# Storing four rows of one image by transfers of 98, 10, 8, 6, 4 and 2 channels

## The chip, the core and the metric

The kernel runs on one core of a Trainium2 chip. The metric is the device time of one execution in microseconds (us); the kernel before took 126.87 us as the median of 3 runs (126.73 to 127.43). A core has a matrix engine (PE, with its weight loads PEld), two elementwise engines (DVE, ACT), a general one (POOL), a sequencer (SP) that here only issues transfers, and 16 DMA engines that move the data between device memory (HBM) and the on-chip buffer. SP and ACT issue stores, each on its own DMA queue: q1 belongs to SP, q10 to ACT; q0 belongs to POOL, which issues loads that also cast.

## The reference

A 3x3 convolution with padding 1 over 16 images of 64 input channels, 64 x 64 pixels, into 128 output channels, all in float32:

```
for kh in range(3):
    for kw in range(3):
        output[b, co] += weight[co, ci, kh, kw] * x_pad[b, ci, kh:kh+h, kw:kw+w]
```

The inputs are 16.8 MB and 0.3 MB, the output is 33.6 MB.

## The kernel before

The images are taken in eight pairs, `p` = 0 to 7; the 64 channels of two images fill the 128 partitions. A pair is computed in four blocks, `blk` = 0 to 3, of 16 output rows each. In each block PE makes three groups of products per image (L141): `U`, `A` and `Bt`. ACT copies `U` out of the accumulators (L155), and DVE adds `A` to it for the even output rows (L164) and `Bt` for the odd ones (L167). The sums go into `ots[0]` and `ots[1]`, the two output tiles of the pair, one an image: 128 partitions (output channels) of 16 KB, which are 64 rows of 256 bytes.

The pairs' inputs come by loads on POOL's queue (L58, six of them) and on SP's (L42, L46, L48); POOL also makes sums of input rows (L67). The last load is issued at 48.1 us.

What matters here is how the outputs leave. When block 3 of a pair is done, SP stores `ots[0]` whole (2 MB, L97); the store of `ots[1]` is kept in the list `held` and issued by ACT in the next block, after its copies of `U`. Only the last pair is stored in two halves, after blocks 1 and 3. Each of these 18 stores has 128 partitions, and each partition's bytes are one packet of a DMA engine: 16 KB, or 8 KB in the last pair. Each DMA engine gets 8 packets of every store.

Each engine, SP and ACT too, runs its instructions in the order of the program, so an instruction that waits holds all behind it. A transfer reports its landing on a semaphore. The layer that builds the program has eight of these for the transfers of SP and ACT, here called 0 to 7, and hands them out in turn in program order; a transfer that gets a semaphore for a second or third time waits, before it is issued, until the earlier transfer with the same one has landed. In the kernel before, 24 transfers share them: the six loads of SP take 0 to 5, pair 0 takes 6 and 7, pair 1 takes 0 and 1, and so on to pair 5 with 0 and 1, pair 6 with 2 and 3, and pair 7 with 4, 5, 6 and 7.

Of the kernel before, what the change touches and what calls it, by code (L numbers as in the profile page):

```python
# [12 lines left out]
@with_exitstack  # L13
def kernel(
    ctx: ExitStack,
    tc: tile.TileContext,
    x: bass.AP,
    weight: bass.AP,
    out: bass.AP,
):  # L20
    nc = tc.nc
    B, CI, H, W = x.shape
    CO = weight.shape[0]
    assert H == 64 and W == 64 and CI == 64 and CO == 128 and B % 2 == 0
    NP = B // 2
    RB = 8

    keep = tc.keep_in_program_order
    x_rows = x.rearrange("b c h w -> (b c) h w")
    out_rows = out.rearrange("b co h w -> b co h w")  # L30
    w_flat = weight.rearrange("co ci kh kw -> co (ci kh kw)")

    const = ctx.enter_context(tc.tile_pool(name="const", bufs=1))
    psum = ctx.enter_context(tc.tile_pool(name="psum", bufs=8, space=bass.MemoryType.PSUM))
    xpool = ctx.enter_context(tc.tile_pool(name="xpool", bufs=5))
    opool = ctx.enter_context(tc.tile_pool(name="opool", bufs=8))
    spool = ctx.enter_context(tc.tile_pool(name="spool", bufs=3))
    upool = ctx.enter_context(tc.tile_pool(name="upool", bufs=4))


    w_raw = const.tile([CO, CI * 9], F32)
    nc.sync.dma_start(w_raw, w_flat)  # L42
    x0 = opool.tile([128, H, W], F32, tag="ot", name="x0")
    cuts = [(0, 18), (18, 34), (34, 50), (50, 64)]
    for lo, hi in cuts:
        nc.sync.dma_start(x0[:, lo:hi, :], x_rows[0:128, lo:hi, :])  # L46
    x1 = opool.tile([128, H, W], F32, tag="ot", name="x1")
    nc.sync.dma_start(x1, x_rows[128:256, :, :])  # L48
    ident = const.tile([128, 128], F16)
    make_identity(nc, ident)  # L50
    w16 = const.tile([CO, CI * 9], F16)
    keep(nc.gpsimd.tensor_copy(w16, w_raw))  # L52

    xs = {p: xpool.tile([128, H, W], F16, tag="xs", name="xs") for p in (0, 1)}

    def load(p):
        xs[p] = xpool.tile([128, H, W], F16, tag="xs", name="xs")
        keep(nc.gpsimd.dma_start(xs[p], x_rows[128 * p : 128 * p + 128, :, :]))  # L58

    ss = {}  # L60

    def sums(eng, p, src, lo, n):
        if p not in ss:
            ss[p] = spool.tile([128, H // 2, W], F16, tag="ss", name="ss")
        v = src.rearrange("p (j i) c -> p j i c", i=2)
        keep(
            eng.tensor_add(  # L67
                ss[p][:, lo : lo + n, :], v[:, lo : lo + n, 0, :], v[:, lo : lo + n, 1, :]
            )
        )  # L70


    Wt = const.tile([128, 5, 3, CO], F16)
    G0, G21, G1, G01, G2 = range(5)

    def wrow(i):
        return Wt[:, i, :, :].rearrange("p t c -> p (t c)")

    for kh, g in ((1, G1), (2, G2), (0, G0)):
        wp = psum.tile([128, 512], F32, tag="acc", name="wp")  # L80
        for k in range(3):
            t = 3 * kh + k
            for q in (0, 64):
                nc.tensor.matmul(wp[q : q + 64, k * CO : k * CO + CO], w16[:, t::9], ident)  # L84
        keep(nc.scalar.copy(wrow(g), wp[:, 0 : 3 * CO]))  # L85
    keep(nc.gpsimd.tensor_sub(wrow(G21), wrow(G2), wrow(G1)))  # L86
    keep(nc.gpsimd.tensor_sub(wrow(G01), wrow(G0), wrow(G1)))  # L87
    for p in range(2, 5):
        load(p)
    for n, (lo, hi) in enumerate(cuts):  # L90
        sums(nc.vector, 0, x0, RB * n, RB)
        keep(nc.scalar.copy(xs[0][:, lo:hi, :], x0[:, lo:hi, :]))  # L92

    held = []

    def store(eng, p, b2, ot, lo, hi):
        return eng.dma_start(  # L97
            out_rows[2 * p + b2, :, lo:hi, :],
            ot.rearrange("p j i c -> p (j i) c")[:, lo:hi, :],
        )  # L100

    for p in range(NP):
        if p + 1 < NP:
            for lo in (0, 16):
                sums(nc.gpsimd, p + 1, x1 if p == 0 else xs[p + 1], lo, 16)
        if p > 0 and p + 4 < NP:
            load(p + 4)
        ots = [
            opool.tile([128, H // 2, 2, W], F32, tag="ot", name="ot") for _ in range(2)
        ]  # L110
        for blk in range(4):
            j0 = blk * RB

            def group(wi_rows):

                tiles = [
                    psum.tile([128, RB, W], F32, tag="acc", name="acc") for _ in range(2)
                ]
                n = 3 * len(wi_rows)
                i = 0  # L120
                for wi, off in wi_rows:
                    for kw in (1, 0, 2):
                        c_lo, c_hi = max(0, 1 - kw), min(W, W + 1 - kw)
                        for b2 in range(2):
                            p0 = 64 * b2
                            lo, hi = j0, j0 + RB
                            if off is None:
                                rhs = ss[p][p0 : p0 + 64, lo:hi, c_lo + kw - 1 : c_hi + kw - 1]
                            else:
                                while 2 * lo + off < 0:  # L130
                                    lo += 1
                                while 2 * (hi - 1) + off > H - 1:
                                    hi -= 1
                                first = 2 * lo + off
                                last = 2 * (hi - 1) + off
                                rhs = xs[p][
                                    p0 : p0 + 64,
                                    first : last + 1 : 2,
                                    c_lo + kw - 1 : c_hi + kw - 1,
                                ]  # L140
                            nc.tensor.matmul(  # L141
                                tiles[b2][:, lo - j0 : hi - j0, c_lo:c_hi],
                                Wt[p0 : p0 + 64, wi, kw, :],
                                rhs,
                                start=i == 0,
                                stop=i == n - 1,
                            )
                        i += 1
                return tiles

            U = group([(G1, None)])
            us = []
            for b2 in range(2):
                ut = upool.tile([128, RB, W], F32, tag="ut", name="ut")
                keep(nc.scalar.copy(ut, U[b2]))  # L155
                us.append(ut)
            if p == 0:
                for lo in {2: (0, 16), 3: (32, 48)}.get(blk, ()):
                    keep(nc.scalar.copy(xs[1][:, lo : lo + 16, :], x1[:, lo : lo + 16, :]))  # L159
            while held:  # L160
                keep(store(nc.scalar, *held.pop(0)))
            A = group([(G21, 1), (G0, -1)])
            for b2 in range(2):
                nc.vector.tensor_add(ots[b2][:, j0 : j0 + RB, 0, :], A[b2], us[b2])  # L164
            Bt = group([(G01, 0), (G2, 2)])
            for b2 in range(2):
                nc.vector.tensor_add(ots[b2][:, j0 : j0 + RB, 1, :], Bt[b2], us[b2])  # L167
            parts = {3: (0, 64)} if p < NP - 1 else {1: (0, 32), 3: (32, 64)}
            if blk in parts:
                lo, hi = parts[blk]  # L170
                store(nc.sync, p, 0, ots[0], lo, hi)
                held.append((p, 1, ots[1], lo, hi))
    while held:
        keep(store(nc.scalar, *held.pop(0)))

# [29 lines left out]
```

## Time and profile before

| | |
|---|---|
| median of 3 runs | 126.87 us |
| profiled execution | 126.71 us, of which its span is 124.9 us |
| PE | 106.1 us busy (85%), its last matmul before 112 us |
| DVE | 83.3 us (67%) |
| ACT | 44.6 us (36%) |
| POOL | 37.4 us (30%) |
| q1 (SP), q10 (ACT), q0 (POOL): share of the 16 DMA engines' span | 41.3%, 31.6%, 24.6% |
| HBM read and written | 17.07 MB and 33.55 MB |

The span runs from the first to the last instruction; 1.8 us of the execution's time lie around it. The page cuts the span into 40 equal slices and gives, for each engine, the busy share of a slice in tenths. For the DMA engines it gives the mean share of the 16. Windows of the trace give the same for stretches that one chooses, and the list of transfers gives the time from the issue of a transfer to its landing.

### The profile page before, as it was taken

How to read it: one execution, taken by the hardware profiler on the slowest of the kernel's cores; microseconds unless marked ns; L12 is line 12 of the kernel's file. 1: busy time of each engine (PE TensorE's matmuls, PEld its weight loads, DVE VectorE, ACT ScalarE, POOL GpSimd, SP SyncE). 2: the span in 40 equal slices, each digit the busy share in tenths (PEclk: the TensorE clock that was granted, in tenths of full speed). 3: DMA queues.
4: the chain of work that ended last, by engine and by line, in shares of the span. 5: the costliest groups of instructions: out<-in, count | busy, mean ns of one | idle time of the engine just before them, and what ended most of it. 6: DMA issues, size and time to landing. Idle time of an engine off the chain costs nothing.

```text
span 124.9 us, 2410 instructions
## 1 busy us (share of the span) xinstructions
PE 106.1 (85%) x978; PEld 53.9 (43%) x978; DVE 83.3 (67%) x132; ACT 44.6 (36%) x76; POOL 37.4 (30%) x29
## 2 busy tenths in 40 slices
PE   0489999999999999999999999999999999970000
PEld 0334455554555545455554554555545555430000
DVE  0066777877787778777877878887887787771000
ACT  4396379533333333333333333333333333320000
POOL 2293079995019401290005800084000000000000
PEclk9999999999999999999999999999999999996555
DMA  4999999999999999999999999999999999999992
GB/s 115 332 434 420 283 215 215 218 226 362 378 359 370 328 349 380 359 338 344 367 378 354 338 357 373 428 425 425 425 436 425 441 420 430 420 417 425 428 404 102
DMA packets 4330, 44.48 MB, mean 356 GB/s; under 512 B 480, under 2 KB 480, under 8 KB 1120
## 3 DMA queue, kind: packets, MB, share of 16 engines
q1 hardware_dynamic: 2160, 21.27, 41.3%
q10 hardware_dynamic: 1296, 16.78, 31.6%
q0 software_dynamic: 864, 6.29, 24.6%
q8 instruction: 7, 0.11, 0.3%
q14 instruction: 3, 0.02, 0.0%
HBM read 17.07 MB, written 33.55 MB: 405 GB/s over the span
## 4 chain that ended last, share of the span: by engine, by line
PE 83%; DMA 4%; DVE 2%; issue 1%; DVEq 0%; SPq 0%
PE acc L141 83%; DMA x<-in_x_dram 4%; DVE ot L164 1%; DVE ss L67 1%; DVE ot L167 0%; DVEq L200 0%; SPq L42 0%; DVEq L164 0%
## 5 line engine op out<-in xcount | busy, mean ns | idle before, releaser
L141 PE MATMUL acc<-xs,Wt 64*128 64x504 f16 (+3 forms) x768 | 88.9, 378 | 0.0
L141 PEld LDWEIGHTS <-Wt 64*128 64x128 f16 x960 | 52.8, 95 | 52.8 <-issue 3.3
L155 ACT COPY ut<-acc 128x512 f32<-128x512 f32 x64 | 34.4, 590 | 61.6 <-issue 42.8
L164 DVE TENSOR_TENSOR ot<-acc,ut 128x512 f32<-128x512 f32 x64 | 41.2, 686 | 22.3 <-PE acc L141 19.2
L167 DVE TENSOR_TENSOR ot<-acc,ut 128x512 f32<-128x512 f32 x64 | 41.2, 685 | 0.0
L67 POOL TENSOR_TENSOR ss<-xs 128x1024 f16<-128x1024 f16 x12 | 25.2, 2123 | 26.4 <-DMA xs<-in_x_dram 15.9
L141 PE MATMUL acc<-ss,Wt 64*128 64x504 f16 (+1 forms) x192 | 27.0, 384 | 1.0 <-DVE ss L67 1.0
L67 DVE TENSOR_TENSOR ss<-x 128x512 f16<-128x512 f32 x4 | 3.0, 741 | 7.3 <-DMA x<-in_x_dram 7.3
L58 POOL DMA_DIRECT2D xs<-in_x_dram x6 | 3.5, 580 | 11.6 <-PE acc L141 11.6
L67 POOL TENSOR_TENSOR ss<-x 128x1024 f16<-128x1024 f32 x2 | 4.7, 2366 | 5.8 <-DMA x<-in_x_dram 5.8
L84 PE MATMUL wp<-ident,w 128*64 128x128 f16 x18 | 1.3, 328 | 4.4 <-POOL w L52 4.4
L92 ACT CAST xs<-x 128x1024 f16<-128x1024 f32 (+2 forms) x4 | 4.1, 1058 | 0.2 <-DMA x<-in_x_dram 0.2
L159 ACT CAST xs<-x 128x1024 f16<-128x1024 f32 x4 | 4.0, 1059 | 0.0
L84 PEld LDWEIGHTS <-w 128*64 128x64 f16 x18 | 1.1, 210 | 4.4 <-POOL w L52 4.4
L85 ACT CAST Wt<-wp 128x384 f16<-128x384 f32 x3 | 1.2, 489 | 3.1 <-PE wp L84 3.1
L86 POOL TENSOR_TENSOR Wt<-Wt 128x384 f16<-128x384 f16 x1 | 1.4, 1439 | 1.7 <-ACT Wt L85 1.7
L85 ACT ACT_TABLE_LOAD x1 | 1.3, 1283 | 0.7 <-PEq L189 0.7
L52 POOL CAST w<-w_raw 128x576 f16<-128x576 f32 x1 | 0.7, 665 | 2.4 <-DMA w_raw<-in_weight_dram 2.4
L87 POOL TENSOR_TENSOR Wt<-Wt 128x384 f16<-128x384 f16 x1 | 1.4, 1353 | 0.0
masks.py:199 POOL TENSOR_SCALAR_AFFINE_SELECT ident<-ident 128x128 f16<-128x128 f16 x1 | 0.3, 293 | 0.1
masks.py:197 POOL MEMSET ident<- 128x128 f16 x1 | 0.2, 205 | 0.3 <-POOLq L189 0.3
L189 POOL MEMSET const-float32-0.0<- 128x1 f32 x1 | 0.1, 98 | 0.2 <-issue 0.2
(3 smaller groups left out, 0.3 us busy)
## 6 DMA issues: line engine op xcount, KB each, us to landing
out_dram<-ot SPq DMA_DIRECT2D x7, 2048.0 KB, 20.7
out_dram<-ot ACTq DMA_DIRECT2D x7, 2048.0 KB, 20.9
xs<-in_x_dram POOLq DMA_DIRECT2D x6, 1024.0 KB, 27.4
x<-in_x_dram SPq DMA_DIRECT2D x1, 2048.0 KB, 13.0
out_dram<-ot SPq DMA_DIRECT2D x2, 1024.0 KB, 12.2
out_dram<-ot ACTq DMA_DIRECT2D x2, 1024.0 KB, 12.0
x<-in_x_dram SPq DMA_DIRECT2D x2, 512.0 KB, 6.0
x<-in_x_dram SPq DMA_DIRECT2D x1, 576.0 KB, 4.8
```

The costliest lines, as they stand in the source:

```text
L58: keep(nc.gpsimd.dma_start(xs[p], x_rows[128 * p : 128 * p + 128, :, :]))
L67: eng.tensor_add(ss[p][:, lo : lo + n, :], v[:, lo : lo + n, 0, :], v[:, lo : lo + n, 1, :])
L84: nc.tensor.matmul(wp[q : q + 64, k * CO : k * CO + CO], w16[:, t::9], ident)
L85: keep(nc.scalar.copy(wrow(g), wp[:, 0 : 3 * CO]))
L86: keep(nc.gpsimd.tensor_sub(wrow(G21), wrow(G2), wrow(G1)))
L87: keep(nc.gpsimd.tensor_sub(wrow(G01), wrow(G0), wrow(G1)))
L92: keep(nc.scalar.copy(xs[0][:, lo:hi, :], x0[:, lo:hi, :]))
L141: nc.tensor.matmul(tiles[b2][:, lo - j0 : hi - j0, c_lo:c_hi], Wt[p0 : p0 + 64, wi, kw, :], rhs, start=i == 0, stop=i == n - 1,)
L155: keep(nc.scalar.copy(ut, U[b2]))
L159: keep(nc.scalar.copy(xs[1][:, lo : lo + 16, :], x1[:, lo : lo + 16, :]))
L164: nc.vector.tensor_add(ots[b2][:, j0 : j0 + RB, 0, :], A[b2], us[b2])
L167: nc.vector.tensor_add(ots[b2][:, j0 : j0 + RB, 1, :], Bt[b2], us[b2])
```

## The change

In pair 5 (`NP - 3`), the store of `ots[0]` leaves out rows 60 to 63, so each of its packets has 15 KB. These four rows, 1 KB in each of 128 partitions, are stored on SP's queue by six transfers of 98, 10, 8, 6, 4 and 2 partitions, written in the program after block 1 of pair 6. The store of `ots[1]` stays whole. No byte is added or left out.

```
-    def store(eng, p, b2, ot, lo, hi):
+    def store(eng, p, b2, ot, lo, hi, c_lo=0, c_hi=CO):
         return eng.dma_start(
-            out_rows[2 * p + b2, :, lo:hi, :],
-            ot.rearrange("p j i c -> p (j i) c")[:, lo:hi, :],
+            out_rows[2 * p + b2, c_lo:c_hi, lo:hi, :],
+            ot.rearrange("p j i c -> p (j i) c")[c_lo:c_hi, lo:hi, :],
         )
...
-            parts = {3: (0, 64)} if p < NP - 1 else {1: (0, 32), 3: (32, 64)}
+            if p == NP - 2 and blk == 1:
+                lo = 0
+                for n in (98, 10, 8, 6, 4, 2):
+                    store(nc.sync, *spread, 60, 64, lo, lo + n)
+                    lo += n
+            cut = (p, blk) == (NP - 3, 3)
+            if cut:
+                spread = (p, 0, ots[0])
+            parts = {3: (0, 60 if cut else 64)} if p < NP - 1 else {1: (0, 32), 3: (32, 64)}
             if blk in parts:
                 lo, hi = parts[blk]
                 store(nc.sync, p, 0, ots[0], lo, hi)
-                held.append((p, 1, ots[1], lo, hi))
+                held.append((p, 1, ots[1], lo, 64 if cut else hi))
```

PE, DVE, ACT and POOL keep their instructions in their order. SP has six more. The end of SP's list in the built program, from the store of pair 5 on, with what each transfer waits for (`DMAHW0` is completion semaphore 0, `DVE` the sums):

```
L97 DMACopy out_0_dram<-ot_1060 128x3840 [waits DMAHW0_49,DVE_49]
L97 DMACopy out_0_dram<-ot_1060 98x256 [waits DMAHW2_49]
L97 DMACopy out_0_dram<-ot_1060 10x256 [waits DMAHW3_49]
L97 DMACopy out_0_dram<-ot_1060 8x256 [waits DMAHW4_49]
L97 DMACopy out_0_dram<-ot_1060 6x256 [waits DMAHW5_49]
L97 DMACopy out_0_dram<-ot_1060 4x256 [waits DMAHW6_49]
L97 DMACopy out_0_dram<-ot_1060 2x256 [waits DMAHW7_49]
L97 DMACopy out_0_dram<-ot_1243 128x4096 [waits DMAHW0_49,DVE_49]
L97 DMACopy out_0_dram<-ot_1429 128x2048 [waits DMAHW2_49,DVE_49]
L97 DMACopy out_0_dram<-ot_1429 128x2048 [waits DMAHW4_49,DVE_49]
```

ACT's store of pair 5 has semaphore 1 as before, that of pair 6 now waits for semaphore 1 instead of 3, and those of pair 7 for 3 and 5 instead of 5 and 7.

## The prediction
> **What bounds the kernel now.** I read the page's chain first. It gives PE 83%, but it ends with the last DVE add at about 112.9 us, and the span is 124.9 us. So the last 12 us belong to something that the chain does not follow. The slices and the queues say what it is:
>
> ```profile
> PE   0489999999999999999999999999999999970000
> DMA  4999999999999999999999999999999999999992
> q1 hardware_dynamic: 2160, 21.27, 41.3%
> q10 hardware_dynamic: 1296, 16.78, 31.6%
> q0 software_dynamic: 864, 6.29, 24.6%
> ```
>
> The 16 DMA engines are busy in every slice, and the three queues add up to 97.5% of them. The kernel is bound by its transfers. The waits of SP's queue agree: at the end (L200) it waits for stores alone.
>
> ```profile
> SPq L97 <- DVE ot L167: 105.2, 9, 18.8
> SPq L200 <- DMA out_dram<-ot: 10.9, 6, 4.3
> ```
>
> Next the stores around the change: when each is issued (timeline: start, length), and how long it takes to land (list of transfers, each cut out by a window; the order below is pair 5 by SP and ACT, then the last halves by SP and ACT).
>
> ```profile
> 86.76 0.33 SPq L97 DMA_DIRECT2D out_dram<-ot  x1
> 87.36 0.34 ACTq L97 DMA_DIRECT2D out_dram<-ot  x1
> 99.56 13.14 SPq L97 DMA_DIRECT2D out_dram<-ot  x3
> 100.17 0.34 ACTq L97 DMA_DIRECT2D out_dram<-ot  x1
> ...
> out_dram<-ot SPq DMA_DIRECT2D x1, 2048.0 KB, 17.5
> out_dram<-ot ACTq DMA_DIRECT2D x1, 2048.0 KB, 17.8
> out_dram<-ot SPq DMA_DIRECT2D x1, 1024.0 KB, 11.4
> out_dram<-ot ACTq DMA_DIRECT2D x1, 1024.0 KB, 11.0
> ```
>
> Pair 5 lands at 86.76 + 17.5 = 104.26 us (SP) and 87.36 + 17.8 = 105.16 us (ACT). Pair 6 is issued at 99.56 (the first of the three in that row) and 100.17 us, 4.7 and 5.0 us before that. This lead keeps the DMA engines fed. The last store lands at 112.97 + 11.0 = 123.97 us. Last, windows (length, then five engines, granted clock, DMA share, GB/s):
>
> ```profile
> 0.00:1.70 1.70, 0.00 (x0) 0.00 (x0) 0.00 (x0) 0.97 (x1) 0.70 (x6) 1.00 0.00 0
> 1.70:1.80 0.10, 0.00 (x0) 0.00 (x0) 0.00 (x0) 0.10 (x1) 0.00 (x0) 1.00 0.96 115
> 115.00:120.00 5.00, 0.00 (x0) 0.00 (x0) 0.00 (x0) 0.00 (x0) 0.00 (x0) 0.50 1.01 428
> 120.00:121.00 1.00, 0.00 (x0) 0.00 (x0) 0.00 (x0) 0.00 (x0) 0.00 (x0) 0.50 0.99 418
> 121.00:122.00 1.00, 0.00 (x0) 0.00 (x0) 0.00 (x0) 0.00 (x0) 0.00 (x0) 0.50 0.83 352
> 122.00:123.00 1.00, 0.00 (x0) 0.00 (x0) 0.00 (x0) 0.00 (x0) 0.00 (x0) 0.50 0.49 205
> 123.00:124.00 1.00, 0.00 (x0) 0.00 (x0) 0.00 (x0) 0.00 (x0) 0.00 (x0) 0.50 0.10 41
> ```
>
> Three readings. Stores run at 428 GB/s. The 16 engines do not finish together: the shares after 120 us sum to 2.41 us, so the mean engine ends at 122.4 and the last at about 123.7 us. And a queue that was empty starts 1.0 us after its issue: SP's first load is issued at 0.74 us, and the DMA engines are idle until 1.7.
>
> **The change part by part.** *Fewer bytes in one store, six small ones.* The bytes stay 128 KB, that is 0.31 us of all engines at 428 GB/s. Packets go from 8 of 16 KB to 8 of 15 KB and, on the mean, 8 of 1 KB on each engine. From the trace's packets, 8 KB take 309 ns, 4608 bytes 178 and 2304 bytes 93, a slope of 37 ns per KB and about 8 ns fixed: 8 x 8 ns = 0.06 us on the mean engine. An engine that got none of the small packets would gain 0.30 us, one that got 12 would lose about 0.25. I take 0, between -0.30 and +0.25, because all of this is done by about 104 us and what follows wipes out who was ahead.
>
> Here a rule on which engines get the small packets stands by itself. The Trainium skill, "DMA: Bandwidth & Descriptors", section "Why a DMA increments its semaphore by 16 and not by 1", says that a transfer runs on the largest number of engines up to 16 that divides its partitions, the lowest-numbered ones: 14, 10, 8, 6, 4 and 2 engines here, so that the last two get nothing. The same page's table of latencies calls engines 7 and 15 usually slower; by both rules the change would unload a late engine and be worth about -0.3 us by itself, which no row of this profile can show, since its packets carry no engine numbers.
>
> *Six more issues on SP.* 6 x 0.33 us = 2.0 us on a queue that waits 105 us for DVE. Four can go at once after 86.76 us; the last two wait for semaphores 6 and 7, pair 4's stores, issued at 73.95 and 74.55 us and landing after 20.6 and 20.9 us, at 94.6 and 95.5 us. SP is through with them before its next work at 99.56 us: nothing.
>
> *The semaphores move by six.* This is the term that counts. In the kernel before, pair 6 waits for semaphores 2 and 3, last used by pair 2, long landed. In the changed one it waits for 0 and 1, which **pair 5** used. SP's store of pair 6, ready at 99.56 us, is held until SP's store of pair 5 has landed; ACT's, ready at 100.17, until ACT's has. The lead of 5 us is gone: the engines run dry of pair 5 before pair 6 is known to them.
>
> When do they restart? Pair 5's store lands at 104.26, earlier by its missing bytes on the engine that is last (8 x 37 ns = 0.3 us): 103.96. SP issues at 104.0 (in the kernel before it started 0.03 us after the add that freed it). First packets 1.0 us later, 105.0; on the last of the 16 engines about 105.2, as the first load's packets spread over 0.2 us. What is left is pairs 6 and 7, 8.39 MB / 428 GB/s = 19.6 us, gapless as before, ending at 124.6 to 124.8 us. The last landing came about 0.3 us after its last packet: 124.9 to 125.1. An instruction fetch of 8 KB (packets, at 111.2 us) adds 0.3 if it falls on the last engine: 124.9 to 125.4, middle 125.2, against 123.97. So +1.2 us.
>
> Note what that sum contains: the mean engine loses far more, from about 103.1 us (its end, 122.4, less 19.5) to 105.1, but the last engine, which sets the end, was due at 104.2 and loses only 1.0. After the restart all engines start level.
>
> The unknown in it is the latency from issue to first packet in mid-kernel. Lower bound 0.33 us, the length of the issue itself, before whose end no packet can be known to an engine: +0.5. Upper bound 2.2 us, the first load's whole flight (2.9 us in the page's list) less its bytes (288 KB, 0.7 us), with pair 5 landing at 104.26 without the 0.3 us gain: +2.7. I take 1.0, since that row is the same queue starting from empty engines, though at the program's start.
>
> The same skill page, section "Latency and other measured facts", gives about 0.6 us to the first byte of such a transfer; by that the sum would be +0.8 instead of +1.2. The row above shows 1.0, which decides.
>
> *ACT held.* Behind its held store stand the copies of `U` for block 1 of pair 7, due at 102.66 us. They start when ACT's store of pair 5 has landed (104.6 to 105.2) plus 0.34, about 105.3: 2.6 us late. DVE's adds of that block, due at 103.97, start about 1.9 late, after the first copy; four adds take 2.7 us of a block's 3.2 (PE's 103.65 us of the chain over 32 blocks), so two blocks later some 0.9 is left. The last stores are issued near 113.3 and 113.9 instead of 112.4 and 113.0. The DMA engines have work until 105.1 + 14.7 = 119.8 us by then (pair 6 and half of pair 7), so 5 us of cover: nothing.
>
> Sum: 126.71 + 1.2 = 127.9 us for an execution like the profiled one; the median stands 0.16 above it, so 128.1 us.
>
> **Rivals.** *A short gap, no measurable change.* A restart by 104.5 us or earlier (a start latency of 0.4 us) ends within 0.6 us of before, 126.3 to 127.5. For it: the late engines run to 104.2 anyway. Against it: the 1.0 us row. *Faster.* The unloading counts and the gap does not: 126.87 - 0.3 = 126.6. It decides only if the new packets are there by 104.2 us, when the last engine runs dry, so if pair 5's store lands by 103.2, 0.8 us earlier than I find. *Much slower by ACT.* If the held copies cost 5 us more than I count, the final halves reach dry queues: each further us is one us, 129 to 131. Against it: the 5 us of cover. *Much slower by the small transfers.* Should the 98 partitions go to one engine, 98 x 45 ns = 4.4 us land on it, ahead of pair 6 in its queue: 132. Nothing in the profile excludes it, as all transfers there have 128 partitions. *No wait at all* would need the program not to hold these stores; its list says that it does.
>
> **How the numbers follow.** The held stores with a loss of +0.5 to +2.7 us on the median of 126.87: 0.82, 127.4 to 129.6, with 128.1 inside; the lowest 0.1 us of that, within the bound below, is counted with the next case. Short gap: 0.08. Faster: 0.03. The two much slower: 0.07 together. The range 127.4 to 129.6 leaves the rest out. About 0.5% (0.6 us) is what a measurement of this kernel can tell: faster 0.03, within 0.08, slower 0.89.
>
> **What would show it.** In the profile after: the waits of SP's queue have a wait of L97 for a store of 4 to 5 us; pair 6's stores are issued near 104.0 and 105 us; a window near 103 to 105 us has a DMA share well under 0.9; ACT has a wait of about 5 us there; the shares after 121 us fall off steeply instead of over 3 us; the last store lands near 125.2 us. The prediction is wrong if pair 6 is issued near 99.6 us, if the dip is absent, or if the gap stays but the late engines are others than I think and lose 2 us or more.

## The result and the profile after

The changed kernel took 128.58 us as the median of 4 runs (128.41 to 128.84), beside 126.8 us for the kernel before (126.51 to 127.43). The ratio is 1.0138, with a 95% interval of 1.0104 to 1.0172: slower by about 1.8 us. The profiled execution took 128.67 us, 1.96 more than the profiled one of before; its span is 126.9 us.

The page of the changed kernel, slices and queues:

```profile
PE   0469999999999999999999999999999999920000
DMA  4999999999999999999999999999999949999992
q1 hardware_dynamic: 2332, 21.27, 40.9%
q10 hardware_dynamic: 1296, 16.78, 31.1%
q0 software_dynamic: 864, 6.29, 24.2%
```

The bytes of the three queues are the same; SP's queue has 172 packets more (128 of 1 KB and 44 reports of landing, one from each engine that took part in a small store: 14 + 10 + 8 + 6 + 4 + 2). One slice of the DMA row, the 33rd (101.5 to 104.7 us), has fallen from 9 to 4. Nothing else in that row has changed.

The waits of SP's queue after (who waited for what: us in total, times, longest):

```profile
SPq L97 <- DVE ot L167: 88.9, 8, 19.3
SPq L97 <- DMA out_dram<-ot: 14.1, 3, 8.3
SPq L208 <- DMA out_dram<-ot: 12.6, 6, 3.4
```

The second line is new: SP waits with a store for an earlier store. Its longest wait, 8.3 us, is that of pair 6's store. It began when the last small transfer was out, at about 95.7 us; the part that costs is what lies behind the 99.9 us at which the sums of pair 6 are ready, about 4.1 us.

The issues and flights around it (timeline of SP and ACT, then the list of transfers cut by windows: pair 5 by SP, by ACT, pair 6 by SP):

```profile
87.11 8.53 SPq L97 DMA_DIRECT2D out_dram<-ot  x7
104.04 0.36 SPq L97 DMA_DIRECT2D out_dram<-ot  x1
104.36 0.34 ACTq L97 DMA_DIRECT2D out_dram<-ot  x1
104.79 1.07 ACT L155 COPY ut<-acc 128x512 f32<-128x512 f32 x2 [3.88 <-DMA out_dram<-ot]
...
out_dram<-ot SPq DMA_DIRECT2D x1, 1920.0 KB, 16.9
out_dram<-ot ACTq DMA_DIRECT2D x1, 2048.0 KB, 16.6
out_dram<-ot SPq DMA_DIRECT2D x1, 2048.0 KB, 9.9
```

Pair 5 lands at 87.11 + 16.9 = 104.01 us (SP) and 87.71 + 16.6 = 104.3 us (ACT, issued at 87.71), and pair 6 is issued 0.03 to 0.06 us after each. Its flight is 9.9 us where it was 14.4: the queue is empty when it comes. Windows of the changed kernel (length, five engines, granted clock, DMA share, GB/s):

```profile
102.00:103.00 1.00, 1.00 (x14) 0.47 (x11) 1.00 (x3) 0.00 (x0) 0.00 (x0) 1.00 0.60 240
103.00:104.00 1.00, 1.00 (x12) 0.54 (x10) 0.60 (x2) 0.00 (x0) 0.00 (x0) 1.00 0.26 91
104.00:104.90 0.90, 0.90 (x12) 0.45 (x8) 0.00 (x0) 0.11 (x1) 0.00 (x0) 1.00 0.01 5
104.90:105.00 0.10, 0.10 (x4) 0.07 (x2) 0.00 (x0) 0.10 (x1) 0.00 (x0) 1.00 5.09 2130
...
123.00:124.00 1.00, 0.00 (x0) 0.00 (x0) 0.00 (x0) 0.00 (x0) 0.00 (x0) 0.50 1.07 451
124.00:125.00 1.00, 0.00 (x0) 0.00 (x0) 0.00 (x0) 0.00 (x0) 0.00 (x0) 0.50 0.41 172
125.00:126.00 1.00, 0.00 (x0) 0.00 (x0) 0.00 (x0) 0.00 (x0) 0.00 (x0) 0.50 0.02 8
```

(A packet is counted where it starts, so a short window can show more than 1.) The engines run dry one after another from 102 us on, the last of them just before 104.2 us, and nothing of weight moves until 104.9. Then all start within 0.15 us of each other, the first of them 0.86 us after the start of SP's issue. At the end they also stop together, between 124.5 and 124.8 us by the trace's packets, where in the kernel before they stopped over 2.4 us. But not all: 8 GB/s over the last window is one packet of 8 KB, so one engine goes on alone, to 125.5 us.

### The profile page after: what moved, and what is told of

It reads as the page before. It is cut to its first block, busy times and chain, and to the rows that moved or that the text cites. A ratio compares the mean times of both kernels' runs of the same rounds, so it can differ in the third digit from the quotient of the medians.

```text
span 126.9 us, 2416 instructions
## 1 busy us (share of the span) xinstructions
PE 105.7 (83%) x978; PEld 55.1 (43%) x978; DVE 84.1 (66%) x132; ACT 44.7 (35%) x76; POOL 36.8 (29%) x29
## 4 chain that ended last, share of the span: by engine, by line
PE 81%; DMA 4%; DVE 2%; issue 1%; DVEq 0%; SPq 0%
PE acc L141 81%; DMA x<-in_x_dram 4%; DVE ss L67 1%; DVE ot L164 1%; DVEq L208 0%; DVE ot L167 0%; SPq L42 0%; DVEq L164 0%
## 5 line engine op out<-in xcount | busy, mean ns | idle before, releaser
L141 PEld LDWEIGHTS <-Wt 64*128 64x128 f16 x960 | 53.9, 95 | 52.0 <-issue 3.6
L67 DVE TENSOR_TENSOR ss<-x 128x512 f16<-128x512 f32 x4 | 4.0, 1007 | 6.9 <-DMA x<-in_x_dram 6.8
L86 POOL TENSOR_TENSOR Wt<-Wt 128x384 f16<-128x384 f16 x1 | 0.9, 910 | 1.7 <-ACT Wt L85 1.7
L87 POOL TENSOR_TENSOR Wt<-Wt 128x384 f16<-128x384 f16 x1 | 1.4, 1358 | 0.0
## 6 DMA issues: line engine op xcount, KB each, us to landing
out_dram<-ot ACTq DMA_DIRECT2D x7, 2048.0 KB, 16.6
out_dram<-ot SPq DMA_DIRECT2D x1, 1920.0 KB, 16.9
```

Of the source, the lines that this page charges most:

```text
L67: eng.tensor_add(ss[p][:, lo : lo + n, :], v[:, lo : lo + n, 0, :], v[:, lo : lo + n, 1, :])
L141: nc.tensor.matmul(tiles[b2][:, lo - j0 : hi - j0, c_lo:c_hi], Wt[p0 : p0 + 64, wi, kw, :], rhs, start=i == 0, stop=i == n - 1,)
```

## The experiments

Two theories stand against each other. *Held stores*: the time goes because pair 6's stores wait, through the reused semaphores, until pair 5's have landed, and the queues run dry. *Small transfers*: the 1 KB packets, or their uneven shares on the engines, cost it. The first four kernels below ran beside a kernel before of 126.61 us (28 runs), the last three beside 126.77 us (23 runs).

### Four transfers: the semaphores move by four

```
-                for n in (98, 10, 8, 6, 4, 2):
+                for n in (98, 10, 8, 12):
```

> The same four rows by four transfers of 98, 10, 8 and 12 channels instead of six. The semaphores move by four, so pair 6 waits for those of pair 4 (landed by 95.5 us, before 99.6). Held stores (the loss comes from pair 6 waiting for pair 5 to land): no gap, 126.5 to 127.1 us, pair 6 issued near 99.6 and 100.2 us, no dip of the DMA share at 103 us. Small transfers (1 KB packets or their uneven shares cost the time): still 128 us or more.

Measured: 126.93 us, ratio 1.0042 (1.0025 to 1.0059). Its window from 102 to 106 us (under the next experiment) has no dip, and SP issues pair 6 when its sums are ready:

```profile
99.89 0.36 SPq L97 DMA_DIRECT2D out_dram<-ot  x1
```

Of the 1.4% that the six transfers cost, four of them leave 0.4%.

### Loads that nobody reads: only the semaphores move

```
+            if p == NP - 2 and blk == 1:
+                for n in range(6):
+                    tiny = const.tile([16, W], F32, name=f"tiny{n}")
+                    keep(nc.sync.dma_start(tiny, x_rows[0:16, n, :]))
             parts = {3: (0, 64)} if p < NP - 1 else {1: (0, 32), 3: (32, 64)}
             if blk in parts:
                 lo, hi = parts[blk]
-                store(nc.sync, p, 0, ots[0], lo, hi)
+                keep(store(nc.sync, p, 0, ots[0], lo, hi))
```

Made from the kernel before; `keep` holds SP's order as written.

> The store of pair 5 is whole, as in the kernel before; in place of the six small stores SP issues six loads of 4 KB (16 partitions of 256 bytes) that nothing reads. Only the semaphores move, by six. Held stores: the gap is back, 128.2 to 128.9 us, pair 6 issued near 104.3 and 105 us. Small transfers: 126.7 to 127.1 us, as before.

Measured: 128.69 us, ratio 1.0157 (1.0134 to 1.018), with no small store and no split store at all. The whole loss is there, and pair 6 is issued late as in the change:

```profile
104.11 0.36 SPq L97 DMA_DIRECT2D out_dram<-ot  x1
```

One window each, from 102 to 106 us, of the kernel before, the changed one, the four transfers and the loads, in this order:

```profile
102.00:106.00 4.00, 4.00 (x40) 2.04 (x38) 3.27 (x7) 1.19 (x3) 0.00 (x0) 1.00 1.04 442
```

```profile
102.00:106.00 4.00, 4.00 (x40) 2.01 (x37) 2.19 (x4) 1.07 (x2) 0.00 (x0) 1.00 0.53 215
```

```profile
102.00:106.00 4.00, 4.00 (x42) 1.98 (x38) 3.27 (x6) 1.07 (x2) 0.00 (x0) 1.00 1.02 430
```

```profile
102.00:106.00 4.00, 4.00 (x40) 2.04 (x38) 3.00 (x6) 1.07 (x2) 0.00 (x0) 1.00 0.47 189
```

The last two numbers of a line are the DMA share and GB/s. PE is busy throughout in all four. The transfers stop only in the two kernels whose pair 6 waits for pair 5.

### The six small stores from POOL's queue

```
-                    store(nc.sync, *spread, 60, 64, lo, lo + n)
+                    store(nc.gpsimd, *spread, 60, 64, lo, lo + n)
```

> The six small stores as in the change, but issued by POOL, whose transfers have semaphores of their own, so pair 6 waits for pair 2 as in the kernel before. Held stores: 126.5 to 127.2 us, no gap. Small transfers: 128 us or more.

Measured: 126.85 us, ratio 1.0022 (1.0005 to 1.004); the share from 102 to 106 us is 1.03.

### The six small stores three and three

```
-            if p == NP - 2 and blk == 1:
-                lo = 0
-                for n in (98, 10, 8, 6, 4, 2):
-                    store(nc.sync, *spread, 60, 64, lo, lo + n)
+            now = {(NP - 2, 1): (0, (98, 10, 8)), (NP - 1, 0): (116, (6, 4, 2))}
+            if (p, blk) in now:
+                lo, sizes = now[p, blk]
+                for n in sizes:
+                    keep(store(nc.sync, *spread, 60, 64, lo, lo + n))
```

SP's other stores are kept in order in the same way.

> The six small stores of the change on SP, three (98, 10, 8 channels) before pair 6's store and three (6, 4, 2) after it, the order on SP written out. The semaphores move by three, and pair 6 waits for 5 and 6, long landed. Held stores: 126.5 to 127.1 us. Small transfers: 128 us or more. If the unloading of some engines is worth its 0.3 us, this and the four transfers stand 0.1 to 0.3 us below the kernel before.

Measured: 126.84 us, ratio 1.0025 (1.0007 to 1.0042); the share from 102 to 106 us is 1.03. These are the very transfers of the change, on the same queue, without the hold. The last part of the expectation failed: the unloading is worth nothing that shows, and both kernels (this one and the four transfers) stand 0.2 to 0.3 us above the one before, not below.

### Five transfers: only ACT's store is held

```
-                for n in (98, 10, 8, 6, 4, 2):
+                for n in (98, 10, 8, 6, 6):
```

> The four rows by five transfers of 98, 10, 8, 6 and 6 channels. The semaphores move by five: SP's store of pair 6 waits for pair 4's second store (landed by 95.5 us), only ACT's store of pair 6 waits for pair 5 (SP's store, landed at about 104.0). If the dry queues after SP's held store make the loss: SP's 2 MB bridge 4.9 us, the share of the DMA engines has no dip, 126.6 to 127.2 us, although ACT is held some 4 us as in the change. If the held ACT (its late copies) makes it: 128 us or more.

Measured: 126.82 us, ratio 1.0007 (0.9986 to 1.0028). SP issues pair 6 at its due time, ACT 2.3 us late (in the kernel before ACT's issue comes 0.61 us behind SP's, which would be 101.58 us here):

```profile
100.97 0.36 SPq L97 DMA_DIRECT2D out_dram<-ot  x1
...
100.90 1.07 ACT L155 COPY ut<-acc 128x512 f32<-128x512 f32 x2 [2.09 <-issue]
103.89 0.34 ACTq L97 DMA_DIRECT2D out_dram<-ot  x1
104.33 1.07 ACT L155 COPY ut<-acc 128x512 f32<-128x512 f32 x2 [2.35 <-DVE ot L167]
```

The share from 102 to 106 us is 1.00. So a held store of ACT costs nothing by itself; SP's held store is needed for the loss. (Whether it alone would do was not tried.) The expectation was not met in one point: ACT's store is held 2.3 us, not some 4, and the copies behind it come only 0.3 us late (104.33, where the 3.17 us between two such starts in the kernel before would give 104.07), against 1.8 us in the change. What such late copies cost is not tested here.

### The hold twice

The loads of the second experiment, now in two pairs:

```
-            if p == NP - 2 and blk == 1:
+            if p in (NP - 3, NP - 2) and blk == 1:
```

> The six loads of 4 KB that nothing reads, now twice: before pair 5's store and before pair 6's. Both pairs are held until the pair before has landed. Held stores: two gaps, at about 95 and 105 us, pair 5 issued near 95 and pair 6 near 105.5 us. The second gap starts from engines that the first one has made level, so that none is still working in it: it should cost its full 1.2 to 1.3 us (0.35 landing, 0.03 wake, 0.86 start), against 0.85 for the one gap of the change, and the total is 129.7 to 130.2 us. If a second gap cost nothing more (it is the start of the last part that counts, or ACT's wait): 128.5 to 129 us.

Measured: 130.41 us, ratio 1.029 (1.0249 to 1.0331). The total is 0.2 us above the top of what was expected, but not for the reason given. Windows of this kernel, then ACT and PE behind its first gap:

```profile
93.00:94.00 1.00, 0.00 (x0) 0.00 (x0) 0.00 (x0) 0.00 (x0) 0.00 (x0) 1.00 0.27 104
94.00:95.00 1.00, 0.00 (x0) 0.00 (x0) 0.00 (x0) 0.00 (x0) 0.00 (x0) 1.00 0.03 4
103.00:106.00 3.00, 3.00 (x33) 1.52 (x29) 2.40 (x5) 1.07 (x2) 0.00 (x0) 1.00 0.89 357
125.00:126.00 1.00, 0.00 (x0) 0.00 (x0) 0.00 (x0) 0.00 (x0) 0.00 (x0) 0.50 0.38 156
126.00:127.00 1.00, 0.00 (x0) 0.00 (x0) 0.00 (x0) 0.00 (x0) 0.00 (x0) 0.50 0.06 25
127.00:128.00 1.00, 0.00 (x0) 0.00 (x0) 0.00 (x0) 0.00 (x0) 0.00 (x0) 0.50 0.02 8
...
95.26 2.05 ACT L155 COPY ut<-acc 128x512 f32<-128x512 f32 x4 [7.62 <-DMA out_dram<-ot]
95.89 2.38 PE L141 MATMUL acc<-xs,Wt 64*128 64x512 f16 x9 [2.99 <-ACT ut L155]
```

The first gap is there. PE stands still in it too: ACT is held 7.6 us behind its store, and PE waits 3.0 us for ACT's copies, which it does not in the change. The DMA engines did not go short for it later: their share from 112 to 125 us is 0.99. The second gap is hardly one: a share of 0.89 over 3 us is 0.3 us. Pair 5, itself late, lands for SP at 94.64 + 10.1 = 104.7 us but for ACT only at 94.82 + 13.1 = 107.9, so ACT's packets bridge most of SP's restart. The time went elsewhere: most engines end at 125.4 us, 1.7 after the last of the kernel before, and a single one (0.06 of 16 in the next window) goes on until 127.3. On single engines some packets behind the first restart were long: the 16 KB instruction fetch (879 ns), which runs at 105.9 us here and at 101.0 us, ahead of the gap, in the change, and three store packets of 16 KB with 0.94 to 1.12 us instead of 0.61. Which packets made the last engine late was not separated.

### One even transfer

```
-                for n in (98, 10, 8, 6, 4, 2):
+                for n in (128,):
```

> The four rows by one transfer of all 128 channels: the packets of 1 KB stay, their uneven shares go, the semaphores move by one and nothing is held. If the few tenths that the four and the six unheld transfers cost (126.84 to 126.93 against 126.61 us) come from the fixed part of the small packets: about +0.06 us from 8 x 8 ns, 126.6 to 126.75. If they come from the uneven shares, this is 126.6 too; if from splitting a store at all, 126.85.

Measured: 127.1 us, ratio 1.0021 (1.0001 to 1.0041). The times expected go by a kernel before of 126.61 us; beside 126.77 us they are 0.16 us higher. The result is nearer to the last alternative, a cost of splitting the store at all, but the interval reaches down to nothing. All that can be said is that the unheld kernels with the four rows apart stand 0.1 to 0.4% above the kernel before, with even and with uneven shares; what makes these tenths stays open.

## Why the prediction was right

The forecast was slower, 128.1 us within 127.4 to 129.6; 128.58 came. By its own steps:

- *Bound by transfers.* Right: in every kernel here the end follows the DMA engines.
- *Small transfers, taken as 0.* Right for the change: the loads without any small store cost as much (128.69) as the change (128.58). Without the hold the split costs 0.1 to 0.4%, which is up to and beyond the 0.25 us that was allowed, and nothing was gained: the two rules of the Trainium skill ("DMA: Bandwidth & Descriptors", "Why a DMA increments its semaphore by 16 and not by 1" and "Latency and other measured facts") on which engines are used and which are late gave -0.3 us, which no kernel showed. The page calls its best guess at why engines are late "SWDGE-specific", that is bound to transfers that POOL issues, and POOL's last packet ended at 81.5 us here; the prediction left that out.
- *Six more issues, taken as 0.* Right, though the one of 98 channels occupied SP 0.79 us, not 0.33. The last two went out at 94.57 and 95.41 us, as the waits for pair 4 had it.
- *The semaphores.* Right, and shown from both sides: moved by three, four or five, there is no gap and at most 0.4% is lost; moved by six, with or without the small stores, the gap and the loss are there.
- *The restart.* Landing 104.01 (103.96 was expected), issue 104.04 (104.0), first packets 104.90 (105.0), the last engine's first at about 105.05 (105.2). The latency to the first packet was 0.86 us from the start of the issue and 0.50 us from its end, so the 1.0 us from the start of the first load's issue was a little high. The Trainium skill's 0.6 us to the first byte ("DMA: Bandwidth & Descriptors", "Latency and other measured facts") lies between the two; the page does not say from where it counts. In the note beside the sum, the mean engine's end of pair 5 should read 102.9 us (122.4 less 19.5), not 103.1; nothing else rests on it.
- *The rest, 19.6 us.* 15 of the 16 engines ended at 124.5 to 124.75 us, so 1.1 us after the last of the kernel before: 104.9 + 19.6 = 124.5.
- *The instruction fetch.* This is the term that was mis-sized. It was put at 0 to 0.3 us, the length of its own packet. By the trace's packets it starts at 112.6 us, and the engine that has it ends at 125.51 us, 0.76 after the next. The fetch takes 309 ns, and the store packet behind it on its engine 958 ns instead of 611, so 0.66 us are seen. Two packets ahead of the fetch stands a store packet that took 881 ns (884 with the loads), also instead of 611; what stretched it is not shown. With it the extra is 0.93 us, as much as this engine ends behind the middle of the others (124.57 us). The fetch's place in the last stretch of the queues:

```profile
DMA packets 16, 0.13 MB, mean 262 GB/s; under 512 B 1, under 2 KB 1, under 8 KB 1
q1 hardware_dynamic: 14, 0.11, 50.3%
q10 hardware_dynamic: 1, 0.02, 12.0%
q14 instruction: 1, 0.01, 3.9%
```

  (The changed kernel, 112.5 to 113.0 us: the packets that start there, by queue.) The same was seen with the loads: fetch at 113.2, that engine at 125.55, the next at 124.84. In the kernel before, the fetch fell on an engine that was not the last (123.53 beside 123.67), so it was covered. When the gap had made all engines level, the cover was gone. The packets carry no engine numbers. But from 105 us on they form 16 chains without a gap, each engine has the same store packets, and an engine with 0.66 us more to do cannot be among the 15 that end within 0.3 us of each other. So the fetch's engine is the last one, in both profiles with one gap; a kernel without the fetch was not tried.
- *ACT held, taken as 0.* Right: its wait was 3.9 us (about 5 were expected), and its copies came 1.8 us late (2.6 expected). But its last store was issued at 113.33 us instead of 112.97, no more behind than its store of pair 5 already was (87.71 against 87.36), and the DMA engines' share from 115 to 120 us is 1.03, so they had work.

In the sum: 1.1 us from the restart (1.0 to 1.1 in the prediction) and 0.8 from the fetch (0.15) make 1.9 of the 1.96 us between the two profiled executions. The mechanism was the one forecast; the fetch is the term that was put too low. The rivals fell: the faster one and the one through the small transfers with the kernels that keep these transfers and lose the hold, the short gap with the restart at 104.9 instead of 104.5 us, the one through ACT with the engines that were busy when its last store came.

## What to carry to other kernels

A transfer that is added takes a turn among the completion semaphores, and so changes what every later transfer waits for: before adding one, list the waits of the built program and see how old the transfer is that each new wait names. Where transfers are the bound, a store must be in its queue before the engines have drained the one ahead of it; a wait between the two costs landing, wake and a start of about 0.9 us on every engine at once. And the last engine sets the end, so a small extra on one engine costs nothing while another is later, and shows when all are level (here 0.76 us).

## What was not expected

- The gap idled the engines for some 1.9 us on the mean (a share of 0.53 over 4 us), yet moved the end of most of them by only 1.1 us: their spread at the end fell from 2.4 to 0.25 us.
- An instruction fetch of 8 KB costs its engine 0.66 us or more while stores run, not 0.31. In all nine profiles the store packet behind it took 0.34 to 0.40 us longer than its like.
- The time that an issue occupies SP was not constant. The store of 98 partitions took 0.79 us here, 0.87 as one of three and three, and 1.23 among four or five; those of 2 to 10 partitions took 0.24 to 0.30 us here and up to 1.2 elsewhere. A large store took 0.33 to 0.36 us. What sets it stays open.
